# One order of steps in the rounds of the experts: the activation of the expert in front first, the halves of the next down weights last

## The chip, the cores and the metric

The kernel runs on one core of a Trainium2 chip. A core has TensorE (PE in the profile, with its weight loads as PEld), VectorE (DVE), ScalarE (ACT), GpSimd (POOL) and SyncE (SP), which here only issues DMAs. Each engine works through its own list of instructions in the order in which the program issues them, and waits at an instruction until what it needs is there. The metric is the time of one execution on the device, in microseconds; the kernel before takes 3486.98 us, the median of three runs (3479.33 to 3489.43).

## The reference

A decoder block for 4096 tokens of 1024 values. The change touches only its last part, the experts; the mixer (DeltaNet and retention) before it stays as it is.

```
g_idx = argmax(h @ w_router_group)              # one of 8 groups
top_p, top_i = top_k(softmax(e_logits of that group), 2)
weights = p(group) * top_p / sum(top_p)
# for each of the 64 experts, over its tokens:
gate = xs @ w_gate[e];  up = xs @ w_up[e]       # 1024 -> 256, 256
y    = (silu(gate) * up) @ w_down[e]            # 256 -> 1024
out  = zeros.at[tok].add(y * weights)
return rms_norm(x + out, final_norm)
```

Every token goes to two experts, so its row is summed twice and normalised the second time.

## The kernel before, in words

The experts are worked off in 64 rounds, one loop in `moe`. Each expert has a fixed cap on its tokens, 76 to 256, and a tile holds up to 128 of them: 36 experts have two tiles, 28 have one. The order of the experts (`pairs`, `ORDER`) mixes both. In round e five experts are in work: **c** is expert e, **n** and **m** are the next two, **p** and **q** the two before. A round is a row of steps, each a letter:

- A gathers the token rows of expert e+3 (GpSimd, L1571); M scales the rows of m (ScalarE, L1575).
- B and H turn the first and the second tile of n: 8 transposes on TensorE (L1582) into two PSUM buffers `tr`, and two evictions to `xT` on VectorE (L1584). There are two such buffers in all.
- C and I are the products with the gate and the up weights of c, 32 matmuls each (L1652, `g` and `u`). I also has SyncE fetch later gate and up weights (L1460). N takes the tanh of g (ScalarE, L1661).
- E is the activation of p: two products on VectorE (L1666, L1667), the rounded half `hh` on ScalarE (L1668), the remainder `hl` on VectorE (L1669).
- J splits the down weights of c, which the next round uses: `dh` on ScalarE (L1468) and the remainder `dl` on VectorE (L1469), twice each. Then SyncE fetches the down weights of e+2 into the buffer that this frees (L1463).
- O is the down product of p, for each tile two halves of 12 matmuls (L975 to L977, `y`), each evicted by ScalarE as `ys` (L1595). There are two PSUM buffers `y`.
- F gathers the rows that are already in the output (GpSimd, L1598). D adds q's `ys` to them (VectorE, L1606), takes squares (ScalarE, L1611), the root (VectorE L1615, GpSimd L1616) and a gain row (ScalarE, L1619). G normalises (VectorE, L1623 and L1624) and scatters (GpSimd, L1627).
- L does side work on VectorE, in some rounds only.

A step only issues its instructions; they start when their engine has come to them and their inputs are there. So a row of letters sets the order within each engine, and steps on different engines overlap as far as the data lets them. Nothing else plans the order here: one string of letters does it, with another for the two rounds after the last expert.

```
for o in LOOP if e < NEXP else TAIL:
    do, f = steps[o]
    if do:
        f()
```

Of the kernel before, what the change touches and what calls it, by code (L numbers as in the profile page):

```python
# [915 lines left out]

LOOP, TAIL = "AFCDNBEGIMHJLO", "BLCEFDGHIMNAOJ"
MIX = 'sb bs sb bs sb sb bs bs sb bb bs bb sb bb'.split()  # L920
CAPS = [256, 232, 212, 196, 188, 180, 176, 168, 160, 156, 152, 148, 144, 140, 136, 134, 132, 130,
        128, 128, 124, 120, 118, 116, 112, 108, 104, 100, 96, 92, 84, 76]
# [918 lines left out]
```

## Time and profile before

| what | us |
|---|---|
| median of three runs (range) | 3486.98 (3479.33 to 3489.43) |
| the profiled execution | 3483.95 |
| its span | 3482.0 |
| TensorE busy in the span | 3382.3 (97%) |
| VectorE, ScalarE, GpSimd busy | 2160.8, 1492.9, 1010.6 |
| first product of round 0 to that of round 63 | 2537.56 to 3443.80 |

How to read it: busy time of an engine is an average over parts of the program with different limits. The experts stand in the last quarter of the span. What holds an engine up there is read from the timeline and the waits of that stretch, not from the shares of the whole.

### The profile page before, as it was taken

Reading aid. Unit: us, or ns where it says so; the run is one execution under the profiler, and the core shown is the slowest. Engines: PE = TensorE matmul, PEld = TensorE weight load, DVE = VectorE, ACT = ScalarE, POOL = GpSimd, SP = SyncE. Lnnn points to the kernel's source line nnn. Section 1 sums busy time; section 2 is a strip of 40 time slices with the busy share of each in tenths; the row PEclk is TensorE's granted clock in tenths of the full one; section 3 lists DMA queues with packets and bytes.
Section 4 is the critical chain, followed back from the end, with each engine's and each line's share of the span. In section 5 each row is a group of like instructions: output and inputs, shape, how many; then the busy total and the mean of one; then the engine's idle time right before and its main releaser. Section 6 shows DMA issues by size and latency. Waiting matters only on the chain. (4 is left out here: it accounts for less than half of the span.)

```text
span 3482.0 us, 65321 instructions
## 1 busy us (share of the span) xinstructions
PE 3382.3 (97%) x24377; PEld 3102.6 (89%) x24377; DVE 2160.8 (62%) x5718; ACT 1492.9 (43%) x3322; POOL 1010.6 (29%) x1320
## 2 busy tenths in 40 slices
PE   7999999999999999999999999999999999999996
PEld 6989999999999999999999988888888888888885
DVE  5785576576467566656655734444556677767775
ACT  4444243233333333333332323222255667766775
POOL 1322222232232322322222211111224344444543
PEclk9999999999999999999999999999999999999998
DMA  8675445454544545454554444323378898999995
GB/s 270 225 247 183 162 159 197 159 190 170 182 168 169 179 150 201 159 179 166 181 183 162 145 156 137 123 102 110 132 230 289 285 312 294 311 323 333 336 320 189
DMA packets 393422, 710.98 MB, mean 204 GB/s; under 512 B 52704, under 2 KB 272528, under 8 KB 393104
## 3 DMA queue, kind: packets, MB, share of 16 engines
q1 hardware_dynamic: 356736, 622.03, 52.6%
q0 software_dynamic: 34976, 84.20, 6.7%
q8 instruction: 193, 3.16, 0.4%
q14 instruction: 125, 1.02, 0.1%
q10 hardware_dynamic: 1392, 0.56, 0.1%
HBM read 606.19 MB, written 131.99 MB: 212 GB/s over the span
## 5 line engine op out<-in xcount | busy, mean ns | idle before, releaser
L248 PE MATMUL acc<-wq,hh 128*128 128x256 f32 (+1 forms) x2560 | 744.7, 291 | 16.6 <-DVE gs L281 6.8
L250 PE MATMUL acc<-wq,hl 128*128 128x256 f32 (+1 forms) x2560 | 722.4, 282 | 1.8 <-DVE hl L326 1.8
L249 PE MATMUL acc<-wq,hh 128*128 128x256 f32 (+1 forms) x2560 | 723.2, 283 | 0.2 <-DVE wq L145 0.2
L248 PEld LDWEIGHTS acc<-wq,hh 128*128 128x128 f32 x2560 | 486.2, 190 | 23.8 <-DVE gs L281 9.0
L250 PEld LDWEIGHTS acc<-wq,hl 128*128 128x128 f32 x2560 | 484.5, 189 | 2.6 <-DVE hl L326 2.6
L249 PEld LDWEIGHTS acc<-wq,hh 128*128 128x128 f32 x2560 | 486.1, 190 | 0.7 <-DVE wq L145 0.7
L236 PE MATMUL acc<-hh,wq 128*128 128x512 f32 x768 | 317.7, 414 | 0.0
L238 PE MATMUL acc<-hh,wq 128*128 128x512 f32 x768 | 301.6, 393 | 0.0
L237 PE MATMUL acc<-hl,wq 128*128 128x512 f32 x768 | 301.0, 392 | 0.0
L1652 PEld LDWEIGHTS g<-xT,gu 128*128 128x128 f32 x2048 | 270.3, 191 | 13.2 <-DVE xT L1584 3.4
L1652 PE MATMUL g<-xT,gu 128*128 128x128 f32 (+30 forms) x2048 | 275.6, 293 | 1.5 <-DVE xT L1584 1.5
L1652 PE MATMUL u<-xT,gu 128*128 128x128 f32 (+30 forms) x2048 | 275.6, 293 | 0.0
L1652 PEld LDWEIGHTS u<-xT,gu 128*128 128x128 f32 x2048 | 265.9, 191 | 1.9
L274 DVE SCALAR_TENSOR_TENSOR cv<-xin,pcol,cv 128x512 f32<-128x512 f32 x288 | 216.4, 751 | 73.4 <-ACT cv L272 66.6
L282 POOL TENSOR_TENSOR gs<-gs,nrow 128x256 f32<-128x256 f32 x128 | 98.1, 766 | 448.1 <-DVE gs L281 413.7
L1627 POOL DMA_INDIRECT out_dram<-xg,mi x100 | 130.8, 1308 | 189.0 <-DVE ss L1623 96.4
L975 PE MATMUL y<-dh,hh 128*128 128x512 f32 (+16 forms) x400 | 164.5, 411 | 21.7 <-ACT ys L1595 13.9
L1595 ACT ACTIVATE ys<-y,mf 128x512 f32<-128x512 f32 (+22 forms) x200 | 134.0, 681 | 115.8 <-PE y L977 115.1
L849 POOL TENSOR_TENSOR rqk<-rqk,rb 128x256 f32<-128x256 f32 x128 | 115.3, 901 | 222.6 <-DVE rb L848 132.3
L1598 POOL DMA_INDIRECT xg<-out_dram,mi x97 | 100.5, 1036 | 263.8 <-PE tr L1582 48.4
L238 PEld LDWEIGHTS acc<-hh,wq 128*128 128x128 f32 x768 | 144.2, 188 | 33.0
L291 POOL TENSOR_TENSOR ss<-ss,ex 128x2 f32<-128x2 f32 x128 | 101.4, 792 | 236.8 <-DVE ss L290 203.7
(377 smaller groups left out, 7942.4 us busy)
## 6 DMA issues: line engine op xcount, KB each, us to landing
wq<-wsp SPq DMA_DIRECT2D x420, 512.0 KB, 5.8
gu<-in_w_gate_dram SPq DMA_DIRECT2D x128, 512.0 KB, 6.4
gu<-in_w_up_dram SPq DMA_DIRECT2D x128, 512.0 KB, 7.9
dn<-in_w_down_dram SPq DMA_DIRECT2D x64, 1024.0 KB, 9.5
xi<-in_x_dram SPq DMA_DIRECT2D x64, 512.0 KB, 5.0
wsp<-wq SPq DMA_DIRECT2D x60, 512.0 KB, 4.4
mixed<-mx SPq DMA_DIRECT2D x128, 128.0 KB, 2.7
xi<-mixed SPq DMA_DIRECT2D x32, 512.0 KB, 4.7
```

What stands on the lines that cost most here:

```text
L236: nc.tensor.matmul(a, wh[:, s], hh[:, k, :], start=(k == 0), stop=False)
L237: nc.tensor.matmul(a, wh[:, s], hl[:, k, :], start=False, stop=False)
L238: nc.tensor.matmul(a, wl[:, s], hh[:, k, :], start=False, stop=(k == KC - 1))
L248: nc.tensor.matmul(a[:, :n], hh[:, k, s], wh[:, :n], start=(k == 0), stop=False)
L249: nc.tensor.matmul(a[:, :n], hh[:, k, s], wl[:, :n], start=False, stop=False)
L250: nc.tensor.matmul(a[:, :n], hl[:, k, s], wh[:, :n], start=False, stop=(k == KC - 1))
L274: nc.vector.scalar_tensor_tensor(cv, xin[:, j:j + T], tap(j), cv, op0=OP.mult, op1=OP.add)
L849: nc.gpsimd.tensor_tensor(o.rearrange("p h s d -> p (h s d)"), o.rearrange("p h s d -> p (h s d)"), b.rearrange("p h s d -> p (h s d)"), o ...
L975: nc.tensor.matmul(out, a.hi, b.hi, start=(i == 0), stop=False)
L1595: nc.scalar.activation(self.y[:R, s], y[:R], AF.Copy, scale=self.f[:R, WT, self.n:self.n + 1])
L1627: so = nc.gpsimd.indirect_dma_start(out=orow, out_offset=self.idx(0), in_=self.xg[:self.G], in_offset=None, bounds_check=S - 1, oob_is_err ...
L1652: nc.tensor.matmul(o[:, b, :R], self.w.gu[k // 4][:, k % 4, i * DE + b * P:i * DE + b * P + P], self.xT[:, k, :R], start=(k == 0), stop=(k ...
```

## The change

One string is written in another order. E moves from behind the turn B to the place behind A, ahead of F, C and D. J moves from behind H to the end, behind L and O. The last two rounds (TAIL) keep their order.

```
-LOOP, TAIL = "AFCDNBEGIMHJLO", "BLCEFDGHIMNAOJ"
+LOOP, TAIL = "AEFCDNBGIMHLOJ", "BLCEFDGHIMNAOJ"
```

TensorE's list is the same before and after. What VectorE has in round 44 before, from the second sum of q (the expert with tiles of 128 and 16 rows) to the remainders of the down weights; `ss` and the number behind a name are buffers:

```order
L1606 TENSOR_TENSOR xg_29733<-ys,xg_29733 16x1024
L1615 TENSOR_SCALAR ss_36872<-ss_36872 128x1
L1584 TENSOR_TENSOR xT<-tr,pcol_24673 128x4x128 x2
L1666 SCALAR_TENSOR_TENSOR h<-h,g 128x2x124
L1667 TENSOR_TENSOR h<-h,u 128x2x124
L1669 TENSOR_TENSOR hl<-h,hh 128x2x124
L1623 TENSOR_SCALAR ss_36865<-ss_36865,mf 128x1
L1624 SCALAR_TENSOR_TENSOR xg_29732<-xg_29732,ss_36865,g 128x1024
L1623 TENSOR_SCALAR ss_36872<-ss_36872,mf 128x1
L1624 SCALAR_TENSOR_TENSOR xg_29733<-xg_29733,ss_36872,g 128x1024
L1584 TENSOR_TENSOR xT<-tr,pcol_24673 128x4x16 x2
L1469 TENSOR_TENSOR dl<-dn,dh 128x1024 x2
```

After, from the remainders that round 43 now ends with to the norm of q:

```order
L1469 TENSOR_TENSOR dl<-dn,dh 128x1024 x2
L1666 SCALAR_TENSOR_TENSOR h<-h,g 128x2x124
L1667 TENSOR_TENSOR h<-h,u 128x2x124
L1669 TENSOR_TENSOR hl<-h,hh 128x2x124
L1606 TENSOR_TENSOR xg_29732<-ys,xg_29732 128x1024
L1615 TENSOR_SCALAR ss_36871<-ss_36871 128x1
L1606 TENSOR_TENSOR xg_29733<-ys,xg_29733 16x1024
L1615 TENSOR_SCALAR ss_36878<-ss_36878 128x1
L1584 TENSOR_TENSOR xT<-tr,pcol_24673 128x4x128 x2
L1623 TENSOR_SCALAR ss_36871<-ss_36871,mf 128x1
L1624 SCALAR_TENSOR_TENSOR xg_29732<-xg_29732,ss_36871,g 128x1024
L1623 TENSOR_SCALAR ss_36878<-ss_36878,mf 128x1
```

The remainders `dl` of the round before and the activation (L1666 to L1669) now stand ahead of q's sums (L1606) and ahead of the evictions of n's first tile (L1584, 128 columns).

ScalarE, before, from the evictions of q's two tiles in round 43 to those of p in round 44:

```order
L1595 ACTIVATE ys<-y,mf 128x512 x2
L1595 ACTIVATE ys<-y,mf 16x512 x2
L1611 ACTIVATE g,ss_36865<-xg_29732 128x1024
L1619 ACTIVATE g<-fn,mf 128x1024
L1611 ACTIVATE g,ss_36872<-xg_29733 128x1024
L1619 ACTIVATE g<-fn,mf 128x1024
L1661 ACTIVATE h<-g 128x2x124
L1668 ACTIVATE hh<-h 128x2x124
L1575 ACTIVATE xg_29726<-xg_29726,mf 128x1024
L1468 ACTIVATE dh<-dn 128x1024 x2
L1595 ACTIVATE ys<-y,mf 124x512 x2
```

After, the same stretch up to the halves of round 44:

```order
L1595 ACTIVATE ys<-y,mf 128x512 x2
L1595 ACTIVATE ys<-y,mf 16x512 x2
L1468 ACTIVATE dh<-dn 128x1024 x2
L1668 ACTIVATE hh<-h 128x2x124
L1611 ACTIVATE g,ss_36871<-xg_29732 128x1024
L1619 ACTIVATE g<-fn,mf 128x1024
L1611 ACTIVATE g,ss_36878<-xg_29733 128x1024
L1619 ACTIVATE g<-fn,mf 128x1024
L1661 ACTIVATE h<-g 128x2x124
L1575 ACTIVATE xg_29726<-xg_29726,mf 128x1024
L1595 ACTIVATE ys<-y,mf 124x512 x2
L1468 ACTIVATE dh<-dn 128x1024 x2
```

The halves `dh` (L1468) now follow the evictions `ys` (L1595) instead of standing ahead of them, and `hh` (L1668) stands right behind the halves of the round before, ahead of the squares (L1611).

## Rows read from the trace of the kernel before

**Rows 1.** of the windows, the rounds: us, busy us by engine, clock, DMA share, GB/s
```profile
2537.56:3443.80 906.24, 883.36 (x6008) 778.11 (x6009) 635.85 (x1267) 617.85 (x836) 393.21 (x386) 1.00 0.90 305
```

**Rows 2.** of the waits, weight loads in the rounds: who waited for whom, us, times, longest
```profile
PEld y L975 <- ACT ys L1595: 21.3, 19, 1.9
PEld y L975 <- ACT hh L1668: 8.2, 8, 2.3
```

**Rows 3.** of the timeline, one round: start, us, engine, operation, what ended its wait
```profile
3186.83 3.73 PE L1652 MATMUL g<-xT,gu 128*128 128x124 f32 x32
...
3187.03 0.68 ACT L1595 ACTIVATE ys<-y,mf 16x512 f32<-16x512 f32 x1 [0.71 <-PE y L977]
...
3191.02 1.06 ACT L1611 ACTIVATE g<-xg 128x1024 f32<-128x1024 f32 x1 [0.51 <-DVE xg L1606]
...
3192.20 1.15 ACT L1619 ACTIVATE g<-fn,mf 128x1024 f32<-128x1024 f32 x1
...
3193.26 0.36 ACT L1661 ACTIVATE h<-g 128x248 f32<-128x248 f32 x1
3193.46 0.41 DVE L1666 SCALAR_TENSOR_TENSOR h<-h,g 128x248 f32<-128x248 f32 x1
...
3194.66 1.14 ACT L1575 ACTIVATE xg<-xg,mf 128x1024 f32<-128x1024 f32 x1
...
3194.79 0.42 DVE L1669 TENSOR_TENSOR hl<-h,hh 128x248 fp32r<-128x248 f32 x1 [0.47 <-ACT hh L1668]
...
3194.94 0.67 PE L1582 MATMUL tr<-cst,xg 16*128 16x16 f32 x8
...
3195.53 0.50 PE L975 MATMUL y<-dh,hh 128*124 128x512 f32 x1
...
3198.45 1.74 PE L1652 MATMUL g<-xT,gu 128*128 128x144 f32 x12
```

**Rows 4.** of the timeline, the halves of a down weight and their remainders
```profile
3209.91 1.99 ACT L1468 ACTIVATE dh<-dn 128x1024 fp32r<-128x1024 f32 x2
...
3210.99 2.36 DVE L1469 TENSOR_TENSOR dl<-dn,dh 128x1024 fp32r<-128x1024 f32 x2 [1.11 <-ACT dh L1468]
```

**Rows 5.** of the timeline, a round whose summing expert has two tiles
```profile
3225.80 3.97 PE L1652 MATMUL g<-xT,gu 128*128 128x140 f32 x32
...
3226.19 1.23 DVE L1606 TENSOR_TENSOR xg<-ys,xg 128x1024 f32<-128x1024 f32 x1
...
3231.32 1.28 DVE L1584 TENSOR_TENSOR xT<-tr,pcol 128x512 f32<-128x512 f32 x2
...
3234.39 0.66 PE L1582 MATMUL tr<-cst,xg 12*128 12x12 f32 x8
```

**Rows 6.** of the timeline, the first products of two rounds that follow each other
```profile
3296.07 3.73 PE L1652 MATMUL g<-xT,gu 128*128 128x128 f32 x32
...
3310.51 0.73 PE L1652 MATMUL g<-xT,gu 128*128 128x134 f32 x5
```

**Rows 7.** of the timeline, TensorE at its longest wait there
```profile
3097.25 0.50 PE L975 MATMUL y<-dh,hh 128*128 128x512 f32 x1 [2.09 <-ACT hh L1668]
...
3098.34 0.63 PE L975 MATMUL y<-dh,hh 128*128 128x512 f32 x1
...
3100.47 0.63 PE L977 MATMUL y<-dh,hl 128*128 128x512 f32 x1
```

**Rows 8.** of the windows, the granted clock behind two waits of TensorE
```profile
3098.00:3099.00 1.00, 1.00 (x4) 0.81 (x4) 1.00 (x1) 1.00 (x2) 0.00 (x0) 0.50 1.05 305
...
3418.00:3420.00 2.00, 1.57 (x7) 0.94 (x6) 1.93 (x4) 2.00 (x4) 0.60 (x2) 1.00 0.96 283
```

**Rows 9.** of the timeline, the second of these waits
```profile
3416.55 0.50 PE L975 MATMUL y<-dh,hh 128*128 128x512 f32 x1 [1.93 <-ACT hh L1668]
```

**Rows 10.** of the timeline, the last two down products
```profile
3453.86 0.68 ACT L1595 ACTIVATE ys<-y,mf 84x512 f32<-84x512 f32 x1 [0.69 <-PE y L977]
...
3454.83 0.46 PE L975 MATMUL y<-dh,hh 128*84 128x512 f32 x1 [1.00 <-ACT hh L1668]
```


## Prediction

> **What bounds the kernel now.** I read the windows first: the rounds of the experts, from the first product of round 0 to that of round 63, take 906.24 us, TensorE is busy in 883.36 of them at the full clock, and the DMA engines are 0.90 busy [rows 1]. So TensorE sets the pace of a round, and a change of order can win at most the 22.9 us that it idles there. The view of waits says what that idleness is: a weight load of a down product waits for the eviction ys of an earlier half 19 times, 21.3 us, and for the rounded activation hh 8 times, 8.2 us [rows 2]. The reader sees there just what the edit aims at: ys stands behind the copies dh on ScalarE, hh behind the sums and turns on VectorE.
>
> The timeline of one round says how near the other two engines are. I count from the start of its first product g, at 3186.83, and call the three experts in it q (summed and stored), p (down product), c (gate and up products), with n the next one, which is turned. Here q and n have two tiles of tokens, p and c one. The last ys of q ends at 3187.03 + 0.68, that is at 0.88. TensorE turns the second tile of n at 8.11, starts the down product of p at 8.70, and the next round begins at 11.62, so a tile's down product is 2.92 us, a half of it 1.46 [rows 3]. In the same round the square, the gain, tanh, the scaling, the turn evictions and the activation follow one another on ScalarE and VectorE with few gaps. These two engines run as one chain that ends only just inside TensorE's round.
>
> **The change part by part.** Nothing is added and nothing removed; three steps move.
>
> *The activation (E) goes ahead of the sums (D).* Its four instructions take from 3193.46 to 3194.79 + 0.42, 1.75 us, for 124 columns [rows 3]. It no longer comes late for the down product: the 8.2 us of waits for hh go. But the sums, the squares, the gains and the turn evictions of n all start 1.75 us later, since VectorE and ScalarE work through their lists in order.
>
> *The halves (J) go behind the down product (O).* On ScalarE dh then stands behind the last ys, so it can start at 0.88 of the next round and no earlier. dl starts 1.08 us after dh, and the two dl take 2.36 us [rows 4]. Before, both ran while TensorE did the down product. Now VectorE sits idle from its last turn eviction until the product ends, and pays 0.88 + 1.08 + 2.36 = 4.32 us at the head of the next round, ahead of E and D. The fetch of the next down weight, which SyncE issues when dl is done, moves by the same stretch; the gate and up fetches behind it wait for product u anyway, and the weight has two rounds to arrive. I cost that at nothing. The table loads at every eighth round stand behind this fetch on SyncE too, and are read only behind H; nothing as well. The side work L now falls into VectorE's idle stretch; a small gain that I don't count.
>
> *What is late next.* The chain in the new order for the round of rows 3: dl ends at 4.32, E at 6.07. D for two tiles takes from 3226.19 to 3231.32, 5.13 us (2.57 a tile) [rows 5], to 11.20. The first of the two turn evictions, half of 1.28 us [rows 5], ends at 11.84. Only then has the second tile of n a transpose buffer, since there are two and the first tile fills both. TensorE is there at 8.11, so it waits 3.73 us, and the down product behind it too. Round: 15.35 instead of 11.62.
>
> This holds in every round where q and n have two tiles and p one. From the caps in the code there are 14 of them, 7 with a narrow c (one tile): 7 x 3.73 = 26 us. In the other 7, c has 130 to 188 columns; at 140 TensorE reaches the second turn at 3234.39 - 3225.80 = 8.59 [rows 5], which leaves 3.25; wider ones come later, and the widest hardly wait. I take 2.6 as their mean: 18 us.
>
> Where p and q both have two tiles (19 rounds) ScalarE decides. The second sum starts at 6.07 + 2.57 = 8.64, its square 1.23 later [rows 5], the gain 1.18 after that (3191.02 to 3192.20) and takes 1.15, tanh 0.36, the scaling 1.14 for each tile of the expert after next [rows 3]: 9.87, 11.05, 12.20, 12.56, then 13.70 or 14.84. Only then comes the first ys, 0.68, and the third half of the down product needs its buffer: 14.38 or 15.52. Two halves follow, 2.92: the round is 17.3 or 18.4. Today such a round takes 3310.51 - 3296.07 = 14.44 [rows 6], 2.9 to 4.0 less. Six of the 19 have a wide c, and some today already contain a wait from rows 2, so I take 2.8 each: 53 us.
>
> Where p has two tiles, q and c one (4 rounds), the same chain is 2.57 shorter; I take 1 us each, 4. In the other 26 of these 63 rounds the chain stays inside TensorE's products: nothing. At the end, the last ys but one ends at 3454.54, and the last down product started at 3454.83 [rows 10]. Now 1.08 + 2.36 and E up to hh, about 1.3, come between: 3459.3, so 4 us more.
>
> Chain in all: 26 + 18 + 53 + 4 + 4 = 105 us. Its bounds: less than nothing if the chain hid in full (all of rows 2 given back, -29), and 5.19 us (1.08 + 2.36 + 1.75) in all 63 rounds, +327. The classes put it near 105; the rounds that I counted at nothing and the means I chose could move it by 40 either way.
>
> **The clock.** Waits of this length cost a second time. After TensorE waited 2.09 us at 3097.25, its matmuls took 0.63 us, from 3098.34 to 3100.47 in five steps of 0.43, where 2.92 / 12 = 0.24 is usual [rows 3, 7]; the granted clock of that stretch is 0.50, the level of 1.2 GHz. After a wait of 1.93 us it stayed at 1.00 [rows 8, 9]. About eight matmuls ran slow: 8 x 0.19 = 1.5 us. They are those of the down product, on the path, because ys and the whole chain behind it wait for its end. By the sums above some 29 rounds get a wait over 2.1 us (the 7 narrow ones, 5 of the 7 wide ones, 17 of the 19): 29 x 1.5 = 43 us. Bounds: 0 (the clock holds) and 87 (twice the price). The Trainium skill, "TensorE: Matmul & The Clock Gate", section "A second HAM failure mode: psum-queue depth-cycling", says that short idle spells between groups of matmuls are enough to send the clock back and forth, and that each return is paid for; this speaks against the change. The 2.09 us wait agrees, the 1.93 us one does not, so I don't apply it to every wait; by it all 44 rounds counted above would pay, and the sum would be about 23 us more.
>
> **Sum.** 3483.95 (the profiled execution, 1.95 of it outside the span) + 105 + 43 = 3632. The median of the three runs is 3 us above that execution: 3635.
>
> **The rivals.**
> 1. *Faster: the waits of rows 2 go and nothing takes their place.* The place is the second turn and the third half of the down product; the price is up to 29 us back, 3484 - 25 = 3459 or so. It decides if VectorE is through with E and D before TensorE reaches the second turn at 8.11: without the 5.19 us of dl and E the chain would be there at 6.65. For it: VectorE is busy in 635.85 of 906.24 us only [rows 1]. Against: the idle third is spent waiting inside the chain, and the order of instructions leaves no way round dl. 5%.
> 2. *No change, or little: the later rounds absorb the waits.* A round without two-tile experts could catch up what one with them lost. But TensorE has 883.36 us of work in 906.24 [rows 1], so little is left to catch up in. Within 0.3%: 3%. Half of the chain's price, no clock: 3540, 5%.
> 3. *The chain as worked out, and the clock holds.* For it: only one of the two waits near 2 us made it fall. 3483.95 + 105 + 3 = 3592. 22%.
> 4. *The clock falls behind nearly every wait, and a slow down product lengthens the chain.* 44 rounds x 1.5 = 66, and some rounds twice: 3483.95 + 105 + 75 = 3664, up to 3700 with the means on the high side. 12%.
>
> **How the numbers follow.** The forecast gets 53%. The range from 3575 to 3705 holds it with rivals 3 and 4, down to the chain at 90 without the clock and up to 140 with 80 for it; it leaves out rivals 1 and 2 and the far ends, under 2 in 10. A difference of 0.3% is about the least that a measurement of this kernel can tell from none. Faster by more 5%, within it 3%, slower 92%.
>
> **What would show it.** In the profile after, these 63 rounds should take about 1050 us instead of 906, at a granted clock under 1.00. In the waits a turn (tr) of TensorE that waits for an xT eviction of VectorE should be new, 14 times or more and some 3 us each; the down products should wait for ys longer than now, the hh waits should be gone. VectorE's dl should wait for dh in nearly every round. A round with q, n two tiles and p, c one should be near 15.4 us plus 1.5 for the clock. If the tr waits are missing, or dl comes without waiting, the chain is wrong, and the time will be near that of before; if the rounds are long but the clock stays 1.00, rival 3.

## The result, and the profile after

The changed kernel takes 3674.12 us (median of four runs, 3666.59 to 3680.81) against 3483.17 us before (median of four, the three named above and one more): a ratio of 1.0541, 95% interval 1.0521 to 1.0560. It is slower by 191 us; forecast were 3635 us, in a range from 3575 to 3705. The time lies inside that range, 39 us above the forecast. The profiled execution took 3678.67 us, 194.7 more than that of before.

Nearly the whole difference lies in the rounds of the experts. Their window, from the first product of round 0 to that of round 63 (us, then busy us and instructions of TensorE, its weight loads, VectorE, ScalarE and GpSimd, the granted clock, the DMA share and GB/s):

```profile
2536.60:3634.00 1097.40, 963.88 (x6008) 829.75 (x6008) 629.47 (x1263) 617.77 (x832) 387.50 (x385) 0.91 0.76 252
```

It answers to [rows 1]: 1097.4 us instead of 906.24, 191.2 more. VectorE and ScalarE have as much to do as before (629 and 618 us), TensorE is busy 80 us longer with the same instructions, at a granted clock of 0.91 instead of 1.00, and idles 133.5 us instead of 22.9. The DMA engines fell from 0.90 to 0.76 busy; TensorE waits for none of their transfers in this stretch.

The view of waits of that stretch for TensorE, and the one row of VectorE that belongs to it (us, times, longest):

```profile
PE tr L1582 <- DVE xT L1584: 81.8, 37, 5.1
PE y L975 <- ACT ys L1595: 45.8, 15, 5.2
```

```profile
DVE dl L1469 <- ACT dh L1468: 252.1, 57, 9.0
```

Before, the waits were for ys and hh [rows 2]. Those are rows of the weight loads, of which the one for ys reads 22.2 us, 20 times, when all the rounds are taken in. TensorE's own rows of the kernel before, over the rounds:

```profile
PE y L975 <- ACT ys L1595: 13.9, 15, 1.5
PE y L975 <- ACT hh L1668: 6.8, 8, 2.1
...
PE tr L1582 <- DVE xT L1584: 0.7, 1, 0.7
```

Now a turn waits 37 times for an eviction of VectorE, a kind of wait that hardly existed, and the ys waits are as many (15) but 3.1 us long on average, where they were 0.9. The waits for hh are gone from the rounds. VectorE stands still for 252 us until the halves dh are there. So the activation is no longer late, and what was late next is what the prediction named.

The same round as in [rows 3], round 44, from its first product at 3309.69:

```profile
3309.69 3.73 PE L1652 MATMUL g<-xT,gu 128*128 128x124 f32 x32
3309.89 0.68 ACT L1595 ACTIVATE ys<-y,mf 16x512 f32<-16x512 f32 x1 [1.03 <-PE y L977]
3310.47 1.99 ACT L1468 ACTIVATE dh<-dn 128x1024 fp32r<-128x1024 f32 x2
3311.55 2.36 DVE L1469 TENSOR_TENSOR dl<-dn,dh 128x1024 fp32r<-128x1024 f32 x2 [5.70 <-ACT dh L1468]
...
3313.82 0.41 DVE L1666 SCALAR_TENSOR_TENSOR h<-h,g 128x248 f32<-128x248 f32 x1
...
3315.22 0.42 DVE L1669 TENSOR_TENSOR hl<-h,hh 128x248 fp32r<-128x248 f32 x1 [0.48 <-ACT hh L1668]
3315.55 1.22 DVE L1606 TENSOR_TENSOR xg<-ys,xg 128x1024 f32<-128x1024 f32 x1
...
3320.67 1.28 DVE L1584 TENSOR_TENSOR xT<-tr,pcol 128x512 f32<-128x512 f32 x2
...
3321.41 0.42 PE L1582 MATMUL tr<-cst,xg 16*128 16x16 f32 x4 [3.55 <-DVE xT L1584]
```

The last ys ends at 3310.57, 0.88 into the round. dl starts at 1.86, after an idle time of 5.70 us in which VectorE had nothing else ahead of it, and E ends at 5.95. The first sum starts at 5.86 (it overlaps the remainder), the turn evictions at 10.98, and the second turn at 11.72, after a wait of 3.55 us. Worked out were 11.84 and 3.73. Below, the down product of that round, and its clock in two stretches of 1 us:

```profile
3322.35 0.78 PE L975 MATMUL y<-dh,hh 128*124 128x512 f32 x1
...
3324.21 0.63 PE L976 MATMUL y<-dl,hh 128*124 128x512 f32 x1
...
3326.57 0.39 PE L977 MATMUL y<-dh,hl 128*124 128x512 f32 x1
...
3326.80 4.08 PE L1652 MATMUL g<-xT,gu 128*128 128x144 f32 x32
```

```profile
3323.00:3324.00 1.00, 1.00 (x4) 0.79 (x3) 0.89 (x3) 0.05 (x1) 0.26 (x1) 0.50 1.07 376
...
3326.00:3327.00 1.00, 1.00 (x7) 0.82 (x6) 0.86 (x7) 0.00 (x1) 0.69 (x2) 1.00 0.95 315
```

The down product takes 4.45 us (3322.35 to 3326.80) instead of 2.92, 1.53 more, because most of its matmuls run at the 0.50 level, as in [rows 7, 8]. The round is 17.11 us long, 11.62 before; 15.35 + 1.5 was worked out for it.

The end of the last round, as in [rows 10]:

```profile
3644.28 1.25 ACT L1595 ACTIVATE ys<-y,mf 84x512 f32<-84x512 f32 x2
...
3646.50 2.36 DVE L1469 TENSOR_TENSOR dl<-dn,dh 128x1024 fp32r<-128x1024 f32 x2 [0.90 <-ACT dh L1468]
...
3649.57 0.34 ACT L1668 ACTIVATE hh<-h 128x168 fp32r<-128x168 f32 x1 [2.15 <-DVE h L1667]
...
3649.96 0.72 PE L975 MATMUL y<-dh,hh 128*84 128x512 f32 x1 [5.82 <-ACT hh L1668]
```

The last ys but one ends at 3645.53, and the last down product starts 4.43 us later, at 3649.96. The stretch behind the rounds is 4.5 us longer than before (3676.7 - 3634.0 = 42.7 against 3482.0 - 3443.8 = 38.2); 4 were forecast.

### The profile page after: what moved, and what is told of

Same layout as the page of the kernel before. It is cut to its first block, busy times and chain, and to the rows that moved or that the text cites. A ratio compares the mean times of both kernels' runs of the same rounds, so it can differ in the third digit from the quotient of the medians.

```text
span 3676.7 us, 65396 instructions
## 1 busy us (share of the span) xinstructions
PE 3465.4 (94%) x24377; PEld 3156.3 (86%) x24377; DVE 2157.9 (59%) x5718; ACT 1496.0 (41%) x3322; POOL 1007.6 (27%) x1320
## 5 line engine op out<-in xcount | busy, mean ns | idle before, releaser
L1469 DVE TENSOR_TENSOR dl<-dn,dh 128x1024 fp32r<-128x1024 f32 x128 | 151.2, 1223 | 258.0 <-ACT dh L1468 253.0
L975 PE MATMUL y<-dh,hh 128*128 128x512 f32 (+16 forms) x400 | 193.6, 484 | 51.6 <-ACT ys L1595 45.8
L1595 ACT ACTIVATE ys<-y,mf 128x512 f32<-128x512 f32 (+22 forms) x200 | 134.6, 683 | 207.2 <-PE y L977 207.1
L976 PE MATMUL y<-dl,hh 128*128 128x512 f32 (+16 forms) x400 | 184.5, 461 | 0.0
L977 PE MATMUL y<-dh,hl 128*128 128x512 f32 (+16 forms) x400 | 182.5, 456 | 0.0
L1582 PE MATMUL tr<-cst,xg 128*128 128x128 f32 (+21 forms) x800 | 99.6, 261 | 87.2 <-DVE xT L1584 81.8
L1616 POOL TENSOR_TENSOR ss<-ss,ex 128x1 f32<-128x1 f32 x100 | 86.3, 863 | 339.6 <-DVE ss L1615 339.5
```

Of the source, the lines that this page charges most:

```text
L975: nc.tensor.matmul(out, a.hi, b.hi, start=(i == 0), stop=False)
L976: nc.tensor.matmul(out, a.hi, b.lo, start=False, stop=False)
L977: nc.tensor.matmul(out, a.lo, b.hi, start=False, stop=(i == n - 1))
L1469: nc.vector.tensor_tensor(self.dn.lo[:, k], self.raw[:, k], self.dn.hi[:, k].bitcast(F32), op=OP.subtract)
```

## The experiments

Where no other kernel is named, a difference or ratio below is against the kernel before, measured beside the run (medians 3485.52 to 3489.20 us).

Two theories stood against each other at the start. The first, that of the prediction: ScalarE and VectorE form a chain from one ys to the next, J puts its 3.44 us (1.08 + 2.36) and E its 1.75 us into it ahead of the sums, and a fall of the clock comes on top. The second: each move simply costs what it puts ahead of the sums, in proportion.

**One part alone: E first.**

```
-LOOP = "AFCDNBEGIMHJLO"
+LOOP = "AEFCDNBGIMHJLO"
```

> Only the activation E moves to the front; the halves J stay ahead of the down product. Chain theory: the two dl are over before the round begins, so E ends at about 1.8 us and, with two tiles in q, the first turn eviction at 1.8 + 5.1 + 0.6 = 7.5, before TensorE's second turn at 8.1. No turn waits, no waits for hh (8 us back), the waits for ys a little longer, since the squares start later. About the time of before, 3484, within 0.4%, granted clock 0.99. Rival theory, each move costs by the 1.75 and 3.44 us that it puts ahead of the sums: a third of the 190 us, 3548.

Measured: 3510.74 us, ratio 1.0064 (1.0046 to 1.0082): 22 us slower. Both theories miss, the rival by more. The waits of TensorE:

```profile
PE y L975 <- ACT ys L1595: 31.0, 21, 4.7
PE tr L1582 <- DVE xT L1584: 4.6, 6, 2.4
...
PE y L975 <- ACT hh L1668: 1.9, 1, 1.9
```

The waits for hh are gone from the rounds as forecast (the one left is behind them), and turn waits are few. But the ys waits are 31.0 us instead of 13.9 (21 times instead of 15): the squares come later, so the scaling and dh do, and dh stands ahead of ys. I had said "a little longer" of these waits and costed it at nothing. In the profiled execution the rounds are 28.3 us longer: TensorE idles 16.9 us more, and its own work takes 11.4 us more at a granted clock of 0.99, with 7 falls of the clock where there was one.

**The other part alone: J last.**

```
-LOOP = "AFCDNBEGIMHJLO"
+LOOP = "AFCDNBEGIMHLOJ"
```

> Only the halves J move behind the down product; E stays behind the turn B. Chain theory: the head of a round is 4.3 us late, the first turn eviction with two tiles in q comes at 4.3 + 5.1 + 0.6 = 10.1 and hh at about 12, so the down product starts at 12.1, almost as late as in the changed kernel (12.4): 3655, between 3630 and 3680, with waits of TensorE for hh of some 3 us in more than 20 rounds and a granted clock near 0.97. Rival, additive: two thirds of the 190 us, 3610.

Measured: 3643.42 us, ratio 1.0442 (1.0424 to 1.0461): 154 us slower, in the span of the chain theory and 33 us above the rival's figure.

```profile
PE y L975 <- ACT hh L1668: 68.9, 47, 5.2
PE tr L1582 <- DVE xT L1584: 41.6, 36, 4.5
```

TensorE waits for hh in 47 places, which were 8 (more often and shorter, 1.5 us on average, than the forecast had it), and for the turn evictions in 36. So J is the costly part. E alone costs 22 us and J alone 154, which is 176, and the two together 191: they add nearly up, but not in the proportion of what they put ahead of the sums (1.75 to 3.44); the rival falls.

**The turn ahead of the sums.** Is the limit the two transpose buffers or the chain?

```
-LOOP = "AEFCDNBGIMHLOJ"
+LOOP = "AEFCBDNGIMHLOJ"
```

> The changed kernel with the turn B ahead of the sums D and the tanh N. The first turn eviction then comes at about 6.7 us, before TensorE's second turn. If the two transpose buffers were the limit, the 82 us of turn waits and much of the clock would come back: near 3560. Chain theory: VectorE and ScalarE still have the same work in a row between two evictions ys, so the 82 us turn into waits of the down product for ys and of the next products for xT; turn waits near zero, waits for ys over 90 us, time 3620 to 3690.

Measured: 3689.99 us, ratio 1.0572 (1.0550 to 1.0594).

```profile
PE y L975 <- ACT ys L1595: 98.0, 28, 6.1
PE g L1652 <- DVE xT L1584: 45.9, 15, 4.4
...
PE tr L1582 <- DVE xT L1584: 0.9, 1, 0.9
```

The turn waits are gone, 0.9 us instead of 81.8, and not a microsecond is won. What TensorE waited there it now waits for ys (98.0 instead of 45.8) and at the next product (45.9 instead of 0.9). The place of a wait is not its cause: the two transpose buffers are not the limit, and the result is what the chain theory forecast.

**The clock alone.** Small transposes without use fill TensorE's waits in the changed kernel. A first version has 30 in each of 33 rounds, a second one as many as fit into each wait. Of the second, in part:

```
+def fill(k):
+    for i in range(k):
+        nc.tensor.transpose(c.u[:, i % 2, 192:256], ident[:64], ident[:64, :64])
...
+if o == "H" and e in turn_fill:
+    fill(turn_fill[e])          # 7 to 68 of them, in 26 rounds; 5 to 70 between two tiles in 15 more
```

> The changed kernel with 30 small transposes of the identity into an unused part of the buffer u, where TensorE waits in 33 of the rounds (ahead of the second turn, or between the two tiles of a down product). They add 2 to 3 us of work inside waits of 3 to 5 us. If the half clock is what the time lacks beside the 105 us of the chain, the time at half clock falls from 195 us to under 100 and the kernel gains 30 to 60 us: 3615 to 3645. If the half clock costs nothing because the other engines set the pace anyway, the time stays at 3674 or rises.

Measured: 3672.46 us, ratio 1.0524 (1.0502 to 1.0546), which is not told apart from the changed kernel's. Round 44 says why (TensorE's timeline):

```profile
3316.05 2.08 PE L1750 MATMUL u<-cst 64*128 64x64 f32 x30
3319.66 0.42 PE L1582 MATMUL tr<-cst,xg 16*128 16x16 f32 x4 [1.53 <-DVE xT L1584]
...
3320.60 0.50 PE L975 MATMUL y<-dh,hh 128*124 128x512 f32 x1
...
3321.64 0.63 PE L976 MATMUL y<-dl,hh 128*124 128x512 f32 x1
```

30 transposes last 2.08 us, and the wait of 1.53 us that is left is still followed, two microseconds after its end, by slow matmuls (0.63 us). The time at half clock fell only from 195 to 143 us, and the falls from 36 to 27. The experiment was too weak, so the second version:

> The changed kernel with small transposes (0.069 us each, as measured in the run before) where TensorE waits, in each round as many as fit into its wait of the changed kernel less 0.35 us: 41 rounds, 5 to 70 of them. The run before left 1.5 us waits behind its filler, and the clock still fell in 27 places. If the half clock is on the path: time at half clock under 50 us instead of 195, rounds shorter by 40 to 80 us, 3595 to 3635. If the chain of ScalarE and VectorE sets the time whatever TensorE's clock: within 15 us of 3674 with the clock near 1.00.

Measured: 3645.37 us, ratio 1.0447 (1.0431 to 1.0463): about 33 us less than the changed kernel. Its rounds, and TensorE's waits:

```profile
2535.00:3598.70 1063.70, 1027.05 (x7607) 907.04 (x7607) 628.78 (x1263) 617.37 (x832) 384.34 (x385) 0.96 0.78 260
```

```profile
PE tr L1582 <- DVE xT L1584: 23.7, 42, 3.5
PE y L975 <- ACT hh L1668: 5.8, 1, 5.8
...
PE y L975 <- ACT ys L1595: 2.7, 6, 0.6
```

The waits are filled (the wait of 5.8 us is in the round behind the loop), the granted clock is 0.96, and the time at half clock in the rounds 79 us in 17 falls, 116 us less. The rounds are 1063.7 us, 33.7 shorter. So a microsecond less at half clock gave back 0.29 us here: both sides of the expectation miss, the truth is between. The clock is on the path, but only in part. The changed kernel has 191 us more at half clock than the kernel before (194.6 against 3.4); carried on to all of them (an estimate, 0.29 x 191) the clock would be 55 of the 191 us by which its rounds are longer, and 136 would be left to the chain. Where the transposes themselves end after the wait would have ended, they cost time too, so 55 may be low; no run shows by how much.

**A version that beats both?** If dh only fills idle time of ScalarE at the head of a round, and dl stays where it was, E can be early and ys need not wait. K below is the step with the two dh; J keeps dl and the fetch.

```
-LOOP = "AFCDNBEGIMHJLO"
+LOOP = "AEKFCDNBGIMHJLO"      # and, without E in front, "AKFCDNBEGIMHJLO"
```

> The activation first as in the changed kernel, but the rounded halves dh right behind it on ScalarE, at the head of the round, and the remainders dl at their old place ahead of the down product. Chain theory: dh fills ScalarE's wait for the first sum (it delays the square by 0.3 us at most) and no longer stands ahead of ys, dl is out of the head of the round, so E ends at 1.8, the first turn eviction at 7.9, and the third half finds its buffer at 11.0 to 11.7: waits for hh gone, waits for ys down to a third of before: 3460 to 3478. Rival, any activation at the front costs the 22 us it cost alone: 3490 to 3510.

> The kernel before with only dh moved to the head of the round on ScalarE; E stays behind the turn, dl at its old place. The square then waits for dh until 2.9 us instead of 1.4, hh comes at about 9.5 instead of 8.6, later than the down product can start: waits for ys nearly gone, waits for hh up by about 1 us in half of the rounds: 3475 to 3505. Rival, dh ahead of ys is all that costs TensorE time in the kernel before: 3462.

Measured: 3495.33 us, ratio 1.0018 (1.0009 to 1.0027), and 3502.76 us, ratio 1.0040 (1.0026 to 1.0053). The waits of the first:

```profile
PE y L975 <- ACT ys L1600: 9.8, 8, 3.0
PE tr L1587 <- DVE xT L1589: 7.2, 12, 1.7
PE g L1657 <- DVE xT L1589: 4.4, 2, 2.5
PE y L975 <- ACT hh L1673: 3.2, 1, 3.2
```

and of the second:

```profile
PE y L975 <- ACT hh L1673: 18.9, 25, 2.3
PE g L1657 <- DVE xT L1589: 7.9, 12, 0.9
```

In the first the ys waits fell to 9.8 us and the 19 rounds with two tiles in p and q take 282.5 us instead of 291.6. But the 14 with two tiles in q and n and one in p take 183.1 instead of 169.8: the sums are again later there, by E, and turns and products wait. The rounds of that version in one row:

```profile
2539.31:3455.98 916.67, 892.12 (x6009) 786.64 (x6010) 627.92 (x1265) 614.44 (x836) 395.70 (x385) 0.99 0.90 302
```

They are 10.4 us longer than those of the kernel before [rows 1]. TensorE idles 24.6 us, 1.7 more, and is busy 8.8 us longer, with 6 falls of the clock instead of one: what this order loses is nearly all clock, which neither side had priced. Its time is above the chain theory's span and in the rival's, though E does not cost the 22 us that the rival named, but 6. In the second version hh is late as expected, the time lies in the forecast span, and its rival (3462) falls. The chain theory had the direction of each wait right and the sum of the first wrong.

Two more, with E between the sums and the turn, and with J between the two tiles of a down product:

```
+LOOP = "AFCDENBGIMHJLO"                        # the first
...
+if i:                                          # the second, in the down product
+    between()                                  # J, where p has two tiles
```

> The kernel before with the activation E between the sums D and the turn B, and ahead of the tanh, instead of ahead of everything; the halves J at their old place. Chain theory: the sums are not delayed, the first turn eviction ends at about 5.2 + 1.8 + 0.6 = 7.6, just ahead of TensorE's second turn at 8.1 with wide experts and 7.8 with the narrowest, hh is ready at 6.5 instead of 8.6: the 8 us of waits for hh go, the ys waits stay: 3474 to 3486, same or 0.2% faster. Rival, any delay of the turn evictions costs: 3500 or more.

> The kernel before with the halves J between the first and the second tile of a down product of two tiles, and ahead of it as before where there is one tile. Chain theory: the first two ys no longer stand behind dh, so the 21 us of waits of the third half go; dh then holds up the last two ys by up to 1 us and dl ends up to 1.2 us into the next round, ahead of the sums, which gives some of it back as waits for hh or turns: 3465 to 3490. Rival, dl ahead of the sums costs as in the changed kernel whatever its length: 3530 or more.

Measured: 3486.73 us, ratio 1.0007 (0.9998 to 1.0016), no difference; and 3499.64 us, ratio 1.0042 (1.0028 to 1.0056). In the former the waits changed places: for hh 3.5 us are left and for ys 7.5, both less than before, but turns wait 10.6 us, which the expectation had at none. The latter is above the chain theory's span and below the rival's, so both miss. All its ys waits are gone and TensorE waits for hh in their place, 26 times:

```profile
PE y L975 <- ACT hh L1668: 20.5, 26, 2.0
```

None of the orders tried is faster than the kernel before.

## Why the prediction was right

*What bounds.* Right: the round is TensorE's as long as the chain of ScalarE and VectorE ends inside it, and no longer. The run with the turn ahead of the sums bears it out: 81 us of turn waits were taken away, and came back in full elsewhere.

*E ahead of the sums.* The hh waits went, and the sums came later by E's length, as said. Alone that costs 22 us, by way of ys and of the clock, which the prediction did not follow for a J that stays in its place.

*J behind the down product.* Right, and it is the larger part: 154 us alone. dl started at 1.86 of the round, by the sum at 0.88 + 1.08 = 1.96. Two things that the prediction put at nothing, or at a gain, cost something in single rounds. VectorE waited for a table load in the side work L three times for over 2 us (5.8, 2.6 and 6.0); the third time dl started at 3.30 of round 49. In round 43 it started at 4.35, since VectorE was still at the norms and L of the short round before.

*The sum.* The place and the mechanism held, but not every step, and 148 us were forecast where 195 came. By the classes of the prediction, before to after, in us:

| rounds | before | after | more | forecast with the clock |
|---|---|---|---|---|
| q, n two tiles, p one, c narrow (7) | 81.6 | 121.7 | 40.1 | 26 + 10.5 |
| the same, c wide (7) | 88.2 | 119.8 | 31.6 | 18 + 7.5 |
| q, p two tiles (19) | 291.6 | 390.9 | 99.3 | 53 + 25.5 |
| p two, q and c one (4) | 59.9 | 71.3 | 11.4 | 4 |
| the rest (26) | 384.9 | 393.7 | 8.8 | 0 |

The first class, which was worked through in full, is off by 4 us in 7 rounds. The largest part of what is missing, 21 us, is in the 19 rounds: for them the steps gave 2.9 to 4.0 us each, and I took 2.8, below the lower end. The step itself, that ScalarE and the first ys decide there, held only in the nine of them whose n has one tile. In the other ten (and in two of the next class) n has two tiles as well, and TensorE waits at the second turn, as in the first class, before any half of the down product. One round of each kind (33 and 52):

```profile
3143.82 0.63 PE L975 MATMUL y<-dh,hh 128*28 128x512 f32 x1 [4.39 <-ACT ys L1595]
```

```profile
3455.68 1.19 PE L1582 MATMUL tr<-cst,xg 6*128 6x6 f32 x8 [3.63 <-DVE xT L1584]
```

The nine are 4.4 us longer each, the ten 6.0. The 4 rounds and the rest, taken at 1 us and at nothing, hold another 16 (4.5 of them in a single round of the rest), the wide ones 6.

*The clock.* The step was right and its size too small. I counted 29 falls at 1.5 us, the price of the one fall in the kernel before, which lasted 3.4 us. There were 36, and they lasted 194.6 / 36 = 5.4 us each. TensorE's busy time grew by 80.5 us with them, some 2.3 us for each further fall. Not all of that is on the path: by the filler about 55 us in all, against the 43 forecast.

The condition that I set, a wait over 2.1 us, was too strict. All 31 such waits were followed by a fall, but so were five shorter ones, of 1.40 to 2.01 us. And the 44 rounds that the prediction names for a fall behind every wait don't follow from its classes, which hold 37 (7, 7, 19 and 4); with these its 66 us would be 56, and its 23 us more would be 12.

*The rivals.* Faster: no, E and D are not through before TensorE's turn: in round 44 the first turn eviction started at 10.98, and TensorE had been there at 8.11 before. Same: no. Full clock (3592): no, 0.91 in the rounds. The clock behind nearly every wait (3664 to 3700), which I gave 12%: the time came out there and so did its condition, since 36 of TensorE's 39 waits over 0.9 us were followed by a fall. By the filler the clock was then worth less than its 75 us, and the chain more than its 105. So the forecast had the mechanism, and this rival the better number. Both terms of the forecast were too small, and only the width of its range holds the time.

The Trainium skill, "TensorE: Matmul & The Clock Gate", section "A second HAM failure mode: psum-queue depth-cycling", says that short idle spells between groups of matmuls send the clock back and forth. This trace agrees, with the 36 of 39 waits; the prediction had held one wait of 1.93 us against it.

What stays open: the split between chain and clock rests on one step of 116 us at half clock and a straight line beyond it; a filler that holds the clock in full was not tried.

## What to carry to other kernels

When two engines with work to spare both stand in a row between the same two events, their busy shares say little: follow that row once through a round, and compare its end with the bound engine's. A step is best put where its engine waits for the bound engine, as the halves were; taken out of there, it costs time in every round in which the chain has no slack left (here the 37 rounds of the first four classes; the other 26 cost 9 us together). And price a new wait of TensorE twice, once for itself and once for the slow matmuls behind it.

## What the runs showed of the hardware

A wait of TensorE need not be long to be followed by the half clock (0.50, the level of 1.2 GHz), and in these traces its length alone does not tell whether it will be. In the changed kernel one of 1.40 us was:

```profile
3013.35 0.44 PE L1582 MATMUL tr<-cst,xg 40*128 40x40 f32 x4 [1.40 <-DVE xT L1584]
```

```profile
3016.00:3017.00 1.00, 1.00 (x4) 0.75 (x3) 1.00 (x2) 0.46 (x1) 0.73 (x1) 0.50 0.95 287
```

In the version with dh early and E in front one of 3.02 us was not:

```profile
3199.39 0.41 PE L975 MATMUL y<-dh,hh 128*16 128x512 f32 x1 [3.02 <-ACT ys L1600]
```

```profile
3196.00:3204.00 8.00, 4.98 (x31) 3.07 (x30) 7.01 (x20) 6.10 (x10) 4.35 (x5) 1.00 1.07 361
```

In the kernel before one of 2.09 us was and one of 1.93 us was not [rows 7 to 9]; with the filler, one of 1.53 us, behind 2.08 us of small transposes, was. In the changed kernel 36 falls took the clock to 0.50 for 5.4 us each on average. What decides it is not shown.
